# A streaming-encoder block on one core: 19 instead of 12 of 22 gate and up pairs by seven products

## The chip, the cores and the metric

The kernel runs on one core of a Trainium2 chip. A core has a matrix engine (TensorE, PE in the profile, with its weight loads as PEld), a vector engine (VectorE, DVE), an activation engine (ScalarE, ACT), a general engine (GpSimd, POOL) and a sync engine (SyncE, SP) that here only issues DMAs. Each engine runs its instructions in the order in which they stand in its queue. The metric is the device time of one execution in microseconds (us); the lower the better.

## The reference, cut to what matters

The block works on x, 512 tokens of 1024 channels, in float32. It has two token mixers side by side (a gated delta rule with 8 heads, and a convolution), an output projection with a residual, and a feed-forward part. The change concerns the last:

```
h2 = rmsnorm(x, norm2_w[l])
f_gate, f_up = jnp.split(h2 @ ffn_w_gate_up[l], 2, axis=-1)
x = x + (jax.nn.silu(f_gate) * f_up) @ ffn_w_down[l]
return rmsnorm(x, norm_f_w)
```

The hidden width is 2816, which is 22 tiles of 128. One tile of the gate and the tile of up with the same number make a "pair" f, from 0 to 21.

## The kernel before

**Products.** Every float32 weight is split into a high and a low part (`whi`, `wlo`): `unit` (L101) loads a weight tile into `raw` on SP's queue, copies it to `whi` on ScalarE (L111) and subtracts on VectorE to get `wlo` (L112). The activations are split likewise, so that one exact product is three matmuls, `split3` (L121). The tiles raw, whi and wlo have three buffers each (`wp`).

**Stages.** (1) To about 377 us: the input projections, one unit of 8 k blocks after another, with the work of the heads between them. For each head POOL runs a recursion of 15 steps (L502 and L504, tiles `ytm` and `y`) whose result ScalarE takes up at L557 (`YY<-y`) in a later chain of small matmuls. (2) To about 560 us the remaining projections of the mixers. (3) The output projection `tok_mm` (L918) in two halves, `hf` 0 and 1; in the second half it normalizes the token tiles n = 0 to 3 one by one (`norm2`, with two small POOL operations, L952 and L954, for each), and PE transposes them. (4) The gate and up pairs from about 596 to 829 us. (5) The down projection, `two` (L1213) three times and a tail.

**Pairs in two ways.** A pair below F0 = 10 is direct: 8 k blocks of 3 matmuls for the gate, as many for up, each with 512 columns, so 48 matmuls (`col_tile`, L123). A pair from F0 on goes through `pair` (L1129): the gate and up tiles, split in two along k, are four quarter blocks A11, A12, A21, A22; the activations are split in two along k and in two along the tokens; and the 2 x 2 block product is done with seven products of half blocks in place of eight (the scheme of Strassen and Winograd). Each product, `hprod` (L1120), is 4 k blocks of 3 matmuls with 256 columns, so a pair has 84 matmuls. It has four units, of 1024, 1024, 1024 and 512 columns, and writes four PSUM banks `z`. The banks come from two pools: `bank` (pool psw, name w, five banks) and `bank2` (pool psm, name mm, three banks); pairs take four of the first, or one of the first and three of the second, by turns.

**Sums of weights.** Three of the four units load sums of quarter blocks, s1 to s4, which the kernel makes itself in DRAM. For each sum SP issues a copy of a quarter (L192), and POOL issues a DMA that adds another quarter or sum onto it (L196, `accum_op=ALU.add`). The list `feed` holds the order; `feed_one` issues the next copy and, two copies later, the adding DMA. s2 adds s1, and s4 adds s2. `fill` (L200) is called from `unit` while `start_feed` is set: from step 335 of the heads' stage to the last three units of the output projection, and again from pair 1 on.

**Sums of activations.** `todo` (L1074) is a list of eleven steps that make the activation sums (tiles xb) and their high and low parts (th, tl). Two of them stand in each direct pair from f = 1 on (`next_todo`).

**Down sums.** The down projection goes by seven products as well; its weight sums `wsum` are added on POOL in SBUF. Those that are left after stage 3 (four whole ones) are made by `dsums_to` in the direct pairs with odd f: a load issued by POOL into `wst` (L166), four additions on POOL (L172), and a store (L173). `some_operands` splits the finished hidden tiles for the down projection (tiles fh, fl), and for f from 11 on POOL combines two of them (fm<-fm).

Of the kernel before, what the change touches and what calls it, by code (L numbers as in the profile page):

```python
# [20 lines left out]
FF = 22  # L21
# [11 lines left out]
def block_kernel(ctx, tc, a):  # L33
    nc = tc.nc
# [59 lines left out]
                    st.enter_context(tc.issue_after(i))  # L94
            yield

    loads, start_feed, gps_ = [], [False], []

    last = [None]

    def unit(ap, pool=None):  # L101

        aps = ap if isinstance(ap, tuple) else (ap,)
        n = T * len(aps) if isinstance(ap, tuple) else 1024
        raw, hi, lo = ((pool or wp).tile([P, n if pool else 1024], t, name=x)[:, 0:n]
                       for t, x in ((F32, "raw"), (F32R, "whi"), (F32R, "wlo")))
        for i, p in enumerate(aps):
            loads.append(nc.sync.dma_start(raw[:, i * T:(i + 1) * T] if len(aps) > 1 else raw, p))
        if start_feed[0]:
            fill()  # L110
        marked(S.activation(hi, raw, AF.Copy), "unit")  # L111
        marked(V.tensor_tensor(out=lo, in0=raw, in1=hi.bitcast(F32), op=ALU.subtract), "unit")  # L112
        return hi, lo
# [28 lines left out]
    cs = []  # L142
# [2 lines left out]

    FK, F0 = FF // 2, 10
    sums = {n: dram.tile([FF - F0, P, T], F32, name=n, bufs=1) for n in ("s1", "s2", "s3", "s4")}
    gu = {n: a["wgu"][r * FF + F0:(r + 1) * FF][:, :, c * T:(c + 1) * T]  # L150
          for n, r, c in (("A11", 0, 0), ("A12", 0, 1), ("A21", 1, 0), ("A22", 1, 1))}


    feed = [("s1", 0)] + [w for p in range(FF - F0) for w in (("s3", p), ("s2", p), ("s1", p + 1), ("s4", p))]
    feed = [(*w, *{"s1": ("A21", gu["A22"]), "s3": ("A11", gu["A21"]), "s2": ("A11", sums["s1"]),
                   "s4": ("A12", sums["s2"])}[w[0]]) for w in feed if w[1] < FF - F0]
    fed, begun = [], []
# [28 lines left out]
    def feed_one(n=1):  # L186

        for _ in range(n):
            if feed:
                w, p, m, other = feed.pop(0)  # L190
                with tc.issue_after(loads[-1].ins):
                    nc.sync.dma_start(sums[w][p], gu[m][p])  # L192
                begun.append((sums[w][p], other[p]))
        while len(begun) > (2 if feed else 0):
            with tc.issue_after((fed[-1] if fed else last[0]).ins):
                fed.append(nc.gpsimd.dma_start(*begun.pop(0), accum_op=ALU.add, max_dma_last_dim=2048))  # L196

    units, norming = [0], [False]
# [641 lines left out]
    queue.append(rest)  # L840
    nh = 0
    while step() or chains:
        start_feed[0] = count[0] >= 335
        if nh < H and count[0] >= START - 9 + 32 * nh + sum(OTHERS[:nh]):
            chains.append([0, chain(*done[nh])])
            nh += 1
        for c in list(chains):
            if c[0] <= count[0] or not queue:
                with behind():
                    n = next(c[1], None)  # L850
                if n is None:
                    chains.remove(c)
                else:
                    c[0] = count[0] + n
    background()
    for _, sc, e in ended:
        if not sc:
# [60 lines left out]
    def tok_mm(wname, kts, xh, xl, post, between):  # L918


        for hf in range(2):
# [11 lines left out]
            for kp2 in range(nu - tail):  # L933
                w = unit(a[wname][hf, kp2])
                for n in range(NT):
                    part(n, kp2, w)
            start_feed[0] = not hf
            ws = [unit(a[wname][hf, kp2]) for kp2 in range(nu - tail, nu)]
            cs = slice(hf * 512, hf * 512 + 512)
            for n in range(NT):  # L940
# [105 lines left out]
        tt(b[:, t1], b[:, t2], fm[:, t2], ALU.add, G)  # L1046

    def dsums_to(f):
        if f % 2 and rest:
            k, cs = rest.pop(0)  # L1050
            if rest and rest[0][0] == k:
                rest.pop(0)
                cs = slice(0, T)
            r = fs.tile([P, 4, T], F32, name="wst")[:, :, 0:cs.stop - cs.start]
            dsums_load(k, r, nc.gpsimd, cs)
            dsums_add(k, r, cs)


# [23 lines left out]
    def some_operands(f):  # L1082
        if not ff:
            fxs.close()
            ff.append(ctx.enter_context(tc.tile_pool(name="ff", bufs=FK)))
        for _ in range(3 if f < F0 else 2):
            if len(made) <= f:
                operands(len(made))
                made.append(1)

    def next_todo():
        if todo:
            with behind():
                todo.pop(0)()

    for f in range(F0):
        start_feed[0] = f > 0
        dsums_to(f)
        if f > 1:
            pg = psm.tile([P, T], F32, name="mm")  # L1100
            col_tile(pg, a["wgu"][f], hhk, hlk)
        else:
            pg = first[2 * f][0]
            k_loop(*first[2 * f], slice(2 * P, T))
        sg = fq.tile([P, T], F32, name="cw", bufs=2)
        S.activation(sg, pg, AF.Silu)
        if f:
            next_todo()
            pu = psm.tile([P, T], F32, name="mm")
            col_tile(pu, a["wgu"][FF + f], hhk, hlk)  # L1110
        else:
            pu = first[1][0]
            k_loop(*first[1], slice(2 * P, T))
        tt(hidden(), pu, sg, ALU.mult)
        if f:
            next_todo()
        if f > 6:
            some_operands(f)

    def hprod(ps, w, i, x):  # L1120

# [6 lines left out]

    def pair(f):  # L1129

        z = [bank() for _ in range(4)] if f % 2 == 0 else [bank(), bank2(), bank2(), bank2()]
        s = lambda n: sums[n][f - F0]
        w = unit(a["wgu"][f])
        w46 = unit((a["wgu"][FF + f][:, T:], s("s2")))
        hprod(z[0][:, t1], w, 0, B11)
        hprod(z[1][:, t1], w, 1, B21)
# [252 lines left out]
```

## Time and profile before

| | |
|---|---|
| three runs | 941.52, 942.86 (median), 943.43 us |
| the profiled execution | 943.44 us, span 941.7 us, granted clock 0.997 |
| PE busy | 925.4 us (98%), 4952 matmuls |
| VectorE, ScalarE, POOL busy | 740.8, 558.0, 336.8 us |
| moved by DMA | 177.39 MB |

The profile is of one execution. Its own time is 0.58 us above the median of the runs, and 1.7 us above its span. A busy PE in it means that a matmul is in flight; matmuls overlap, so the rate is read from the distance of one start to the next.

### The profile page before, as it was taken

The numbers are of one execution on the slowest core, as the hardware profiler recorded it, in microseconds if no ns is written. First come the engines' busy times: TensorE is split into PE (matmuls) and PEld (weight loads), VectorE is DVE, ScalarE is ACT, GpSimd is POOL, SyncE is SP. The second block draws the span as 40 slices with busy tenths as digits, with TensorE's granted clock in tenths as the row PEclk, the third lists the DMA queues.
The fourth block names the chain that finished last, engine by engine and source line by source line (L and its number), as shares of the span: only waits on it lengthen the run. The fifth ranks groups of instructions, "written<-read, shape, count | busy, mean of one in ns | idle before, by whom it ended". The sixth has DMA issues, their size and how long they took to land.

```text
span 941.7 us, 14545 instructions
## 1 busy us (share of the span) xinstructions
PE 925.4 (98%) x4952; PEld 785.3 (83%) x4952; DVE 740.8 (79%) x1157; ACT 558.0 (59%) x1278; POOL 336.8 (36%) x541
## 2 busy tenths in 40 slices
PE   9999999999999999999999999999999999999996
PEld 6777788878888888888888888988889999988885
DVE  4889898989989899999587643676536877888896
ACT  6696977888778796643555323324324445466545
POOL 0134345253353437544055341245531111133042
PEclk9999999999999999999999999999999999999999
DMA  9333413223123246989898983699797564577654
GB/s 322 113 114 118 131 68 103 86 85 108 73 77 103 93 136 159 335 263 268 284 286 279 285 236 127 205 292 288 257 257 213 184 197 168 186 236 255 213 181 148
DMA packets 78187, 177.39 MB, mean 188 GB/s; under 512 B 10080, under 2 KB 19472, under 8 KB 77088
## 3 DMA queue, kind: packets, MB, share of 16 engines
q1 hardware_dynamic: 66528, 144.89, 44.9%
q0 software_dynamic: 10288, 28.90, 13.3%
q10 hardware_dynamic: 1296, 2.67, 0.7%
q8 instruction: 39, 0.64, 0.3%
q14 instruction: 36, 0.29, 0.1%
HBM read 156.22 MB, written 45.37 MB: 214 GB/s over the span
## 4 chain that ended last, share of the span: by engine, by line
PE 82%; ACT 7%; DVE 3%; issue 1%; POOL 1%; DMA 1%; POOLq 0%; ACTq 0%; DVEq 0%; SPq 0%
PE mm L121 55%; PE w L121 20%; PE b L526 2%; DVE wlo L112 1%; ACT whi L111 1%; PE g L435 1%; PE g L470 1%; PE st L639 1%; PE st L630 1%; PE st L638 1%; PE st L624 1%; PE st L625 0%; ACT Un L473 0%; DVE xs L964 0%; PE b L435 0%
## 5 line engine op out<-in xcount | busy, mean ns | idle before, releaser
L111 ACT ACTIVATE whi<-raw 128x1024 fp32r<-128x1024 f32 (+1 forms) x191 | 196.4, 1030 | 242.6 <-PE mm L121 158.0
L112 DVE TENSOR_TENSOR wlo<-raw,whi 128x1024 fp32r<-128x1024 f32 (+1 forms) x191 | 239.6, 1256 | 86.1 <-ACT whi L111 84.8
L121 PE MATMUL mm<-hh,whi 128*128 128x512 f32 (+1 forms) x688 | 269.7, 392 | 1.2 <-ACT whi L111 0.8
L121 PE MATMUL mm<-hh,wlo 128*128 128x512 f32 (+1 forms) x688 | 264.2, 385 | 0.8 <-DVE wlo L112 0.8
L121 PE MATMUL mm<-hl,whi 128*128 128x512 f32 (+1 forms) x688 | 263.0, 382 | 0.0
L693 DVE SCALAR_TENSOR_TENSOR cps<-c,c31w,cps 128x512 f32<-128x512 f32 x224 | 167.9, 749 | 3.8
L121 PEld LDWEIGHTS mm<-hh,wlo 128*128 128x128 f32 x688 | 130.0, 189 | 25.0 <-DVE wlo L112 1.3
L121 PEld LDWEIGHTS mm<-hh,whi 128*128 128x128 f32 x688 | 130.3, 189 | 22.9 <-ACT whi L111 1.7
L121 PEld LDWEIGHTS mm<-hl,whi 128*128 128x128 f32 x688 | 130.3, 189 | 20.9
L1022 POOL TENSOR_TENSOR fm<-fm 128x256 f32<-128x256 f32 x33 | 28.1, 852 | 117.7 <-DVE s L1022 93.2
L422 DVE SCALAR_TENSOR_TENSOR acc<-mm,c4w,acc 128x511 f32<-128x511 f32 (+2 forms) x72 | 53.0, 740 | 4.3 <-ACT acc L419 4.1
L502 POOL TENSOR_TENSOR ytm<-U,y 128x60 f32<-128x60 f32 (+14 forms) x120 | 36.7, 306 | 51.0 <-DMA U<-sc 42.2
L121 PE MATMUL mm<-yh,whi 128*128 128x512 f32 x128 | 50.6, 396 | 0.0
L121 PE MATMUL mm<-yh,wlo 128*128 128x512 f32 x128 | 49.8, 389 | 0.0
L121 PE MATMUL mm<-yl,whi 128*128 128x512 f32 x128 | 49.8, 389 | 0.0
L121 PE MATMUL w<-hh,wlo 128*128 128x256 f32 x168 | 47.7, 284 | 0.3 <-DVE wlo L112 0.3
L121 PE MATMUL w<-hh,whi 128*128 128x256 f32 x168 | 47.6, 284 | 0.0
L121 PE MATMUL w<-hl,whi 128*128 128x256 f32 x168 | 47.5, 283 | 0.0
L196 POOL DMA_DIRECT2D s<-in_wgu_dram x24 | 22.7, 962 | 64.0 <-DMA s<-in_wgu_dram 64.0
L121 PE MATMUL w<-wlo,fh 128*128 128x512 f32 (+1 forms) x115 | 44.3, 385 | 0.2 <-DVE wlo L112 0.2
L121 PE MATMUL w<-whi,fl 128*128 128x512 f32 (+1 forms) x115 | 44.2, 385 | 0.0
L121 PE MATMUL w<-whi,fh 128*128 128x512 f32 (+1 forms) x115 | 44.2, 385 | 0.0
(346 smaller groups left out, 1937.5 us busy)
## 6 DMA issues: line engine op xcount, KB each, us to landing
raw<-in_win_dram SPq DMA_DIRECT2D x61, 512.0 KB, 3.2
raw<-in_wgu_dram SPq DMA_DIRECT2D x32, 512.0 KB, 3.2
s<-in_wgu_dram SPq DMA_DIRECT2D x48, 256.0 KB, 5.3
raw<-s SPq DMA_DIRECT2D x48, 256.0 KB, 3.6
raw<-wsum SPq DMA_DIRECT2D x44, 256.0 KB, 3.6
raw<-in_wdn_dram SPq DMA_DIRECT2D x33, 256.0 KB, 3.2
s<-in_wgu_dram POOLq DMA_DIRECT2D x24, 256.0 KB, 6.8
s<-s POOLq DMA_DIRECT2D x24, 256.0 KB, 7.2
```

The source lines that it names most:

```text
L111: marked(S.activation(hi, raw, AF.Copy), "unit")
L112: marked(V.tensor_tensor(out=lo, in0=raw, in1=hi.bitcast(F32), op=ALU.subtract), "unit")
L121: marked(PE.matmul(ps, l, r, start=first and i == 0, stop=last and i == 2))
L196: fed.append(nc.gpsimd.dma_start(*begun.pop(0), accum_op=ALU.add, max_dma_last_dim=2048))
L422: marked(V.scalar_tensor_tensor(out=acc[:, s:], in0=ps[:, :T - s], scalar=c4w[:, j, k:k + 1], in1=acc[:, s:], op0=ALU.mult, op1=ALU.add))
L435: PE.transpose(ps[:, n, :], src[:, n, :], ident)
L470: PE.matmul(ps[:, n, :], kT[:, n, :], kT[:, n, :], start=True, stop=True)
L502: G.tensor_tensor(out=tm[:, :, 0:w], in0=U[:, k, :, k + 1:], in1=y[:, :, k:k + 1].broadcast_to([P, NT, w]), op=ALU.mult)
L526: PE.matmul(ps[:, q, 0:w], stationary[:, q, :], moving[:, q, :], start=True, stop=True)
L624: PE.matmul(ps[:, 0, :], kT[:, n, :], Sp, start=True, stop=True)
L693: V.scalar_tensor_tensor(out=acc if k < 30 else cv[i], in0=c[:, k:k + T], scalar=c31w[:, i, k:k + 1], in1=acc if k > 1 else cv[i], op0=ALU ...
L1022: return eng.tensor_tensor(out=out, in0=in0, in1=in1, op=op)
```

## The change

F0 goes from 10 to 3: the pairs 3 to 9 go by seven products too, 19 pairs in all. Around that:

- The list of weight sums grows from 48 to 76. Its order takes two pairs by turns (s3 of two, s2 of two, s1 of the next two, s4 of two). It is issued from step 72 of the heads' stage on, one sum at each unit (`ahead`), and with the last three units of the output projection and those of pair 0 as well.
- Each call of `next_todo` does two steps, with calls in the direct pairs 0 to 2 and one in each `pair`.
- The down sums that are left stand behind pairs 8, 11, 14 and 17.
- The turns of the PSUM banks count from F0, so that the last pair takes four banks of pool w; before, it took one of w and three of mm.

```diff
+        elif ahead[0]:
+            feed_one()
...
-    FK, F0 = FF // 2, 10
+    FK, F0 = FF // 2, 3
...
-    feed = [("s1", 0)] + [w for p in range(FF - F0) for w in (("s3", p), ("s2", p), ("s1", p + 1), ("s4", p))]
+    feed = [("s1", 0), ("s1", 1)] + [(n, p + d + i) for p in range(0, FF - F0, 2)
+                                     for n, d in (("s3", 0), ("s2", 0), ("s1", 2), ("s4", 0)) for i in range(2)]
...
-            with tc.issue_after((fed[-1] if fed else last[0]).ins):
+            with tc.issue_after(fed[-1].ins) if fed else nullcontext():
...
+        ahead[0] = count[0] >= 72
         start_feed[0] = count[0] >= 335
...
-            start_feed[0] = not hf
+            start_feed[0], ahead[0] = not hf, hf
...
-        if f % 2 and rest:
+        if f > 7 and f % 3 == 2 and rest:
...
-            dsums_load(k, r, nc.gpsimd, cs)
+            with tc.issue_after(loads[-1].ins):
+                dsums_load(k, r, nc.gpsimd, cs)
...
-        for _ in range(3 if f < F0 else 2):
+        for _ in range(2):
...
-        if todo:
+        for _ in todo[:2]:
             with behind():
                 todo.pop(0)()
...
-        if f:
-            next_todo()
-        if f > 6:
-            some_operands(f)
+        next_todo()
...
-        z = [bank() for _ in range(4)] if f % 2 == 0 else [bank(), bank2(), bank2(), bank2()]
+        z = [bank() for _ in range(4)] if (f - F0) % 2 == 0 else [bank(), bank2(), bank2(), bank2()]
...
+        next_todo()
```

What this does to the queues is shown at three places. The first is POOL's queue in the heads' stage, between the recursion of head 0 and that of head 1, before (L464 to L486 make the tiles from which the recursion of head 1 starts):

```order
L504 TENSOR_TENSOR y_720<-y_720,ytm_764 128x4
L464 TENSOR_TENSOR ss_1005<-ss_1005,root4_85 128x4
L474 TENSOR_TENSOR Un_1029<-Un_1029,DT_663 128x512
L481 COPY cp_1035<-Un_1029 32x128 x4
L484 TENSOR_SCALAR cc_1036<-cp_1035,cst_76 128x64
L485 TENSOR_SCALAR ct_1037<-cp_1035,cst_76 128x64
L486 TENSOR_TENSOR cc_1036<-cc_1036,ct_1037 128x64
```

The same place after:

```order
L507 TENSOR_TENSOR y_720<-y_720,ytm_764 128x4
L199 DMA s1_125<-in_wgu_dram 128x512 x2
L199 DMA s3_127<-in_wgu_dram 128x512
L467 TENSOR_TENSOR ss_1005<-ss_1005,root4_85 128x4
L199 DMA s3_127<-in_wgu_dram 128x512
L477 TENSOR_TENSOR Un_1029<-Un_1029,DT_663 128x512
L199 DMA s2_126<-s1_125 128x512
L484 COPY cp_1035<-Un_1029 32x128 x4
L487 TENSOR_SCALAR cc_1036<-cp_1035,cst_76 128x64
L488 TENSOR_SCALAR ct_1037<-cp_1035,cst_76 128x64
L489 TENSOR_TENSOR cc_1036<-cc_1036,ct_1037 128x64
L199 DMA s2_126<-s1_125 128x512
```

Six adding DMAs now stand among the steps that lead to the next recursion; in all, 35 of the 76 stand in the heads' stage ahead of the place where POOL's first down sum stood.

The second place is POOL's queue in the second half of the output projection: ss2 is the tile of `norm2`, and the first four of its eight TENSOR_SCALARs belong to the first half. Before:

```order
L952 TENSOR_SCALAR ss2_6029<-ss2_6029 128x1 x5
L954 TENSOR_TENSOR ss2_6029<-ss2_6029,half_81 128x1
L952 TENSOR_SCALAR ss2_6029<-ss2_6029 128x1
L954 TENSOR_TENSOR ss2_6029<-ss2_6029,half_81 128x1
L952 TENSOR_SCALAR ss2_6029<-ss2_6029 128x1
```

After:

```order
L957 TENSOR_SCALAR ss2_6093<-ss2_6093 128x1 x3
L199 DMA s2_126<-s1_125 128x512
L957 TENSOR_SCALAR ss2_6093<-ss2_6093 128x1
L199 DMA s1_125<-in_wgu_dram 128x512
L957 TENSOR_SCALAR ss2_6093<-ss2_6093 128x1
L959 TENSOR_TENSOR ss2_6093<-ss2_6093,half_81 128x1
L199 DMA s1_125<-in_wgu_dram 128x512
L957 TENSOR_SCALAR ss2_6093<-ss2_6093 128x1
L959 TENSOR_TENSOR ss2_6093<-ss2_6093,half_81 128x1
```

Three adding DMAs stand among these, the last of them between token tiles 0 and 1 of the second half.

The third place is PE's queue where the last pair ends and the down projection begins, with what each matmul waits for. The mm or w with 256 columns is the last product of pair 21; the four w with 512 columns are the first four accumulators of the down projection. Before:

```order
L121 MATMUL mm_8747<-hh_92,wlo_8835 128x256
L121 MATMUL w_8889<-whi_8894,fh_7101 128x512 [waits Activation_49]
L121 MATMUL w_8889<-whi_8894,fl_7102 128x512
L121 MATMUL w_8889<-wlo_8895,fh_7101 128x512 [waits DVE_49]
L121 MATMUL w_8890<-whi_8894,fh_7101 128x512
L121 MATMUL w_8890<-whi_8894,fl_7102 128x512
L121 MATMUL w_8890<-wlo_8895,fh_7101 128x512
L121 MATMUL w_8891<-whi_8894,fh_7101 128x512 [waits PE_49]
```

After:

```order
L123 MATMUL w_9223<-hh_92,wlo_9311 128x256
L123 MATMUL w_9365<-whi_9370,fh_6935 128x512 [waits Activation_49]
L123 MATMUL w_9365<-whi_9370,fl_6936 128x512
L123 MATMUL w_9365<-wlo_9371,fh_6935 128x512 [waits DVE_49]
L123 MATMUL w_9366<-whi_9370,fh_6935 128x512 [waits DVE_49]
L123 MATMUL w_9366<-whi_9370,fl_6936 128x512
L123 MATMUL w_9366<-wlo_9371,fh_6935 128x512
L123 MATMUL w_9367<-whi_9370,fh_6935 128x512 [waits DVE_49]
```

Pool w has five banks. With four of them in the last pair, the second, third and fourth accumulator of the down projection take over banks of that pair, and each now waits for VectorE to have read its bank.

3 lines of the change are left out of this document (2 added, 1 removed).

## The prediction

> **What bounds the kernel now.** I read the page first, then the busy time by stage (windows), then PE's timeline at the ends of stages, then the waits.
>
> ```profile
> span 941.7 us, 14545 instructions
> ...
> PE 925.4 (98%) x4952; PEld 785.3 (83%) x4952; DVE 740.8 (79%) x1157; ACT 558.0 (59%) x1278; POOL 336.8 (36%) x541
> ...
> PE 82%; ACT 7%; DVE 3%; issue 1%; POOL 1%; DMA 1%; POOLq 0%; ACTq 0%; DVEq 0%; SPq 0%
> ```
>
> PE is busy 98% of the span, and 82% of the chain that ended last is PE's. The windows are the heads' stage, the end of the output projection with pair 0, the direct pairs 2 to 9, and the pairs 10 to 21 of seven products (columns: length, then busy time of PE, PEld, DVE, ACT, POOL, then clock, DMA share, GB/s):
>
> ```profile
> 44.00:377.00 333.00, 327.03 (x1716) 270.43 (x1717) 300.20 (x566) 270.48 (x821) 145.94 (x343) 0.99 0.33 105
> 560.00:615.00 55.00, 54.68 (x324) 48.33 (x323) 29.43 (x36) 19.49 (x34) 11.13 (x19) 1.00 0.52 167
> 620.80:707.80 87.00, 87.00 (x385) 72.09 (x384) 47.14 (x42) 27.77 (x37) 38.36 (x37) 1.00 0.91 278
> 707.80:828.80 121.00, 121.00 (x1010) 120.96 (x1009) 92.72 (x139) 59.53 (x83) 17.01 (x22) 1.00 0.60 190
> ```
>
> In the two windows of pairs PE never waits. What happens there is worth its matmuls, as long as the others keep up: VectorE has (121.00 - 92.72) / 12 = 2.4 us to spare in a pair of seven products.
>
> **The gain.** PE's timeline has the first matmul of pair 2, of pair 10, of pair 15, of the down projection, and of its third accumulator:
>
> ```profile
> 620.79 0.39 PE L121 MATMUL mm<-hh,whi 128*128 128x512 f32 x1
> 707.83 0.28 PE L121 MATMUL w<-hh,whi 128*128 128x256 f32 x1
> 758.23 0.28 PE L121 MATMUL w<-hh,whi 128*128 128x256 f32 x1
> 828.78 0.40 PE L121 MATMUL w<-whi,fh 128*128 128x512 f32 x1
> 830.17 0.39 PE L121 MATMUL w<-whi,fh 128*128 128x512 f32 x1
> ```
>
> Eight direct pairs take 707.83 - 620.79 = 87.04 us, 10.88 each: 48 matmuls at 0.227 us. Twelve pairs of seven products take 828.78 - 707.83 = 120.95 us, 10.08 each: 84 matmuls at 0.120 us. Not an eighth is gained but 0.80 us of 10.88, since a matmul of half the columns takes more than half the time. Seven pairs change over: 7 x 0.80 = **-5.6 us**, all of it on PE's path.
>
> Each of the 84 needs a weight load of its own, and that is longer than its step:
>
> ```profile
> L121 PEld LDWEIGHTS w<-hh,whi 128*128 128x128 f32 x168 | 32.2, 192 | 0.0
> ```
>
> A load of 192 ns is shown for each 120 ns of matmul, so loads lie beside matmuls and beside each other. [...]
>
> **The bank at the end of the pairs.** The last pair now has four banks of pool w, and the down projection's second to fourth accumulator take them over. VectorE reads them in pair 21 at these times (the sum of z[2], then of z[1]):
>
> ```profile
> 830.04 0.68 DVE L1022 TENSOR_TENSOR fm<-mm,cv 128x512 f32<-128x512 f32 x1
> 830.64 0.68 DVE L1022 TENSOR_TENSOR cw<-cw,mm 128x512 f32<-128x512 f32 x1
> ```
>
> The third accumulator starts at 830.17 now, and its bank is then z[1], read out at 830.64 + 0.68 = 831.32. PE waits 831.32 - 830.17 = **+1.15 us**. The second takes z[0], which was read long before; the fourth takes z[2], free at 830.72, before PE comes to it. No other work of PE is queued ahead, so nothing hides this.
>
> **Down sums beside pairs of seven.** Nothing that the order shows holds POOL's first `wst` load back to pair 8, and I expect POOL to run the four blocks about when it does now: the first beside pairs 0 and 1, the other three at 636, 655 and 676 us, now beside pairs of seven products. Rows of POOL's and VectorE's timelines, two such blocks, then two operations beside the first of them and one with POOL idle:
>
> ```profile
> 613.40 8.00 POOL L172 TENSOR_TENSOR wst<-wst 128x512 f32<-128x512 f32 x4 [1.22 <-DMA wst<-in_wdn_dram]
> ...
> 676.27 6.33 POOL L172 TENSOR_TENSOR wst<-wst 128x512 f32<-128x512 f32 x4 [7.49 <-DMA wst<-in_wdn_dram]
> ```
> ```profile
> 613.66 2.11 DVE L112 TENSOR_TENSOR wlo<-raw,whi 128x1024 fp32r<-128x1024 f32 x1
> 615.70 2.32 DVE L1022 TENSOR_TENSOR xb<-xb,xb 128x1024 f32<-128x1024 f32 x1
> ...
> 755.13 1.23 DVE L112 TENSOR_TENSOR wlo<-raw,whi 128x1024 fp32r<-128x1024 f32 x1 [0.68 <-ACT whi L111]
> ```
>
> A subtraction for wlo takes 2.11 beside POOL's additions and 1.23 alone, 0.9 more; the xb of 615.70 takes 1.1 more than the one of 605.41 that is quoted below. A block of 6.3 to 8.0 us has room for four such operations of VectorE: 0.9 + 3 x 1.1 = 4.2 us lost. Two things cover that: the 2.4 us that VectorE has to spare in a pair, of which 1.9 lie in the block's 8 of 10 us; and its lead, since the wlo of 755.13 is done at 756.36 and PE comes to its pair at 758.23, 1.9 us, and to the matmul that reads wlo two steps of 0.12 later, 2.1. So a block costs 4.2 - 1.9 - 2.1 = 0.2 us. Bounds: 0 if only three operations meet a block, 4.2 - 2.1 = 2.1 a block if the spare time lies elsewhere. For three blocks **+0.6 us**, between 0 and 6.3; nearer to 0, since the spare time is there in every pair.
>
> **The eleven steps of todo**, pressed from six pairs into three. Four joins, four sums and three subtractions at 1.2 us (the xb of 605.41 below) are 13.5, with the first `wst` block 17.7. Beside them VectorE has five wlo (6.2), two fm (1.4) and two fl (0.8) before pair 3 begins at 620.79 + 48 x 0.227 = 631.7.
>
> ```profile
> 605.41 1.22 DVE L1022 TENSOR_TENSOR xb<-hh,hl 128x1024 f32<-128x1024 f32 x1
> 657.39 5.58 DVE L1019 TENSOR_TENSOR fl<-fm,fh 128x256 fp32r<-128x256 f32 x5 [0.48 <-ACT fh L1018]
> ```
>
> With those, 17.7 + 6.2 + 1.4 + 0.8 = 26.1 us of work in 631.7 - 605.4 = 26.3 us: just full. The first of the tiles is read in the third product, 24 x 0.12 = 2.9 us into the pair, which is the cover that is left. I take **+0.3 us**, a little over one more block's worth, between 0 and 2. Without that cover it would be 2.9 more.
>
> **Adding DMAs among POOL's work.** 35 come into the heads' stage, five a head. Their price now, over 48, with POOL's longest wait for a copy, and the slack of the recursion: its last `y` and ScalarE's taking it up, for the heads 1, 3 and 7 (1 has the smallest slack of the heads 1 to 7; the other four lie above that of head 3):
>
> ```profile
> L196 POOL DMA_DIRECT2D s<-in_wgu_dram x24: 800/894/1715, 361.0 to 706.0; - x24
> ```
> ```profile
> POOL s L196 <- DMA s<-in_wgu_dram: 77.6, 16, 13.1
> ```
> ```profile
> 125.10 0.21 POOL L504 TENSOR_TENSOR y<-y,ytm 128x4 f32<-128x4 f32 x1
> ...
> 204.40 0.21 POOL L504 TENSOR_TENSOR y<-y,ytm 128x4 f32<-128x4 f32 x1
> ...
> 358.82 0.21 POOL L504 TENSOR_TENSOR y<-y,ytm 128x4 f32<-128x4 f32 x1
> ```
> ```profile
> 140.97 0.34 ACT L557 ACTIVATE YY<-y,cst 128x64 f32<-128x64 f32 x1
> ...
> 224.38 0.33 ACT L557 ACTIVATE YY<-y,cst 128x64 f32<-128x64 f32 x1
> ...
> 376.29 0.35 ACT L557 ACTIVATE YY<-y,cst 128x64 f32<-128x64 f32 x1
> ```
>
> Five calls at 0.9 us are 4.5 us a head, or 8.6 at 1.7 each, against slacks of 140.97 - 125.31 = 15.7, 19.8 and 17.3 us. POOL has 333 - 146 us free there. So they are hidden: 0. The order of the other engines in this stage is shuffled by it, and PE's idle 333.00 - 327.03 = 6.0 us may move by a third either way: +-2, taken as 0. DMAs are no bound there (share 0.33).
>
> Of the sums, 14 pairs' worth stand ahead of the last normalization in POOL's queue, so pair 3 finds its own, and SP does not wait.
>
> In the output projection's second half one adding DMA stands ahead of token tile 1's normalization:
>
> ```profile
> 587.38 0.30 POOL L952 TENSOR_SCALAR ss<-ss 128x1 f32<-128x1 f32 x1 [3.06 <-ACT sg L950]
> ```
> ```profile
> 579.73 0.33 SPq L108 DMA_DIRECT2D raw<-in_wgu_dram  x1
> ```
> ```profile
> s<-in_wgu_dram SPq DMA_DIRECT2D x48, 256.0 KB, 5.3
> ```
>
> Its copy follows the weight load of 579.73 on SP, so it is issued at 580.1 and lands 5.3 later; POOL's call ends at 586.3, 1.1 us ahead of need: 0, up to 3 if the copy is late.
>
> **Sum.** -5.6 + 1.15 + 0.6 + 0.3 = -3.55 us. Against the profiled 943.44 that is 939.9; the runs' median lies 0.58 lower, so the forecast is 942.86 - 3.55 = **939.3 us**. 0.2% of this time is 1.9 us, about what a measurement can tell from no change.
>
> **Rivals.**
> - *The cover holds everywhere*: neither the down sums nor todo cost PE anything, and the heads' stage loses a little of its idle time: -5.6 + 1.15 - 1 = -5.5, 937.4 us. For it: VectorE's spare time. Chance 0.14; faster.
> - *VectorE becomes the bound in pairs 3 to 8*: the blocks cost half of their bound of 6.3, 3.2 in place of 0.6, and todo 1: -5.6 + 1.15 + 3.2 + 1 = -0.25, 942.6. For it: 26.1 of 26.3 us. Against: one block in three pairs. Chance 0.16, of it 0.13 same and 0.03 slower.
> - *POOL's recursion comes late* (the other side): each of the heads 1 to 7 meets one wait of 13.1 us and calls of 1.7, 21.6 us. It decides from a head's slack on: 5.9 us at head 1, 4.3 at head 7 and 1.8 at head 3; with 0 to 1.8 at the other four, taken as 0.5 each, 14.0 in all. -3.55 + 14.0 = +10.45, 953.3. Against it: a copy is issued two sums ahead of its adding. Chance 0.09; slower.
> - [...] Chance 0.01.
>
> The forecast has 0.60: 0.57 faster, 0.03 same. That makes faster 0.71, same 0.16, slower 0.13. The range goes from below the second case, 936.5, to just above the third, 943.0; what is left out is the fourth, the fifth, and the slower part of the third and some way below 936.5.
>
> **What would show it.** Nineteen pairs at 10.08 us each with PE always busy; PE waiting about 1.15 us for VectorE's cw at the down projection's third accumulator; PE waiting for wlo, if at all, beside POOL's `wst`; ScalarE's `YY` never waiting for POOL. It is wrong if a pair of seven in 631 to 707 takes over 10.4 us, if PE's idle time in the heads' stage grows by over 2 us, or if the transposes of token tile 1 wait for POOL.

## The result, and the profile after

The changed kernel takes 956.39 us (median of 4 runs, 956.05 to 957.72), the kernel before 942.80 beside it (941.52 to 943.43): a ratio of 1.0149, interval [1.0131, 1.0166]. It is slower by about 14 us; the prediction was 3.5 us faster.

The page of the changed kernel (first the span, then busy time by engine, then the chain of waits):

```profile
span 954.9 us, 15285 instructions
...
PE 927.7 (97%) x5204; PEld 797.6 (84%) x5204; DVE 767.6 (80%) x1206; ACT 567.8 (59%) x1297; POOL 365.1 (38%) x569
...
PE 67%; ACT 7%; DVE 7%; DMA 6%; issue 4%; POOL 3%; SPq 0%; POOLq 0%; ACTq 0%; DVEq 0%
```

PE's share of the chain falls from 82% to 67%, and VectorE, DMAs and "issue" take what it lost. PE does not have more to do (927.7 us for 925.4); it waits. Where, PE's timeline tells: the first matmul of the output projection, of the gate and up stage, and of the down projection, first before, then after.

```profile
461.37 0.39 PE L121 MATMUL mm<-yh,whi 128*128 128x512 f32 x1
...
596.36 0.36 PE L121 MATMUL w<-hh,whi 128*128 128x256 f32 x1
```
```profile
467.19 0.39 PE L123 MATMUL mm<-yh,whi 128*128 128x512 f32 x1
...
603.04 0.36 PE L123 MATMUL w<-hh,whi 128*128 128x256 f32 x1
...
842.62 0.40 PE L123 MATMUL w<-whi,fh 128*128 128x512 f32 x1
```

The heads lose 467.19 - 461.37 = 5.8 us; the output projection with the normalization 0.9 (135.85 us for 134.99); the gate and up stage takes 842.62 - 603.04 = 239.6 us, where it took 828.78 - 596.36 = 232.4, so 7.2 are lost where 5.6 were to be gained. The down projection is 0.6 shorter. Before rounding that is 13.2 us in all, the difference of the two spans.

The windows of the changed kernel: the heads' stage, the stretch with the loss in the pairs, and the pairs behind it.

```profile
44.00:377.00 333.00, 323.29 (x1694) 267.91 (x1693) 294.65 (x560) 264.35 (x812) 168.63 (x367) 0.99 0.55 150
...
640.00:710.00 70.00, 63.27 (x482) 61.21 (x482) 47.23 (x61) 26.79 (x39) 27.55 (x24) 0.95 0.86 276
...
710.00:840.00 130.00, 130.00 (x1086) 130.00 (x1085) 102.21 (x154) 64.99 (x91) 15.33 (x20) 1.00 0.55 186
```

From 710 us on PE never waits: the gain is real there. Between 640 and 710 us PE has 482 matmuls where the 130 us behind it have 1086 (585 in 70 us), the granted clock is 0.95, and the DMA engines are busy 0.86 at 276 GB/s, against 0.55 at 186 behind. Those are the pairs 3 to 8 with the down sums of GpSimd (called POOL in the profile) beside them.

Who waits there: ScalarE, which makes whi, for loads of the pairs' sums (three figures: us in total, times, longest), and how long those loads take from issue to landing. Both rows are of 640 to 710 us.

```profile
ACT whi L113 <- DMA raw<-s: 23.2, 9, 6.0
```
```profile
raw<-s SPq DMA_DIRECT2D x23, 256.0 KB, 6.1
```

### The profile page after: what moved, and what is told of

The parts are those of the page before. It is cut to its first block, busy times and chain, and to the rows that moved or that the text cites. A ratio compares the mean times of both kernels' runs of the same rounds, so it can differ in the third digit from the quotient of the medians.

```text
span 954.9 us, 15285 instructions
## 1 busy us (share of the span) xinstructions
PE 927.7 (97%) x5204; PEld 797.6 (84%) x5204; DVE 767.6 (80%) x1206; ACT 567.8 (59%) x1297; POOL 365.1 (38%) x569
## 4 chain that ended last, share of the span: by engine, by line
PE 67%; ACT 7%; DVE 7%; DMA 6%; issue 4%; POOL 3%; SPq 0%; POOLq 0%; ACTq 0%; DVEq 0%
PE mm L123 40%; PE w L123 21%; DMA raw<-s 4%; DVE wlo L114 3%; PE b L529 2%; ACT whi L113 2%; DVE cps L696 1%; DMA s<-in_wgu_dram 1%; POOL ytm L505 1%; DVE acc L425 1%; PE st L642 1%; PE g L438 1%; PE st L641 1%; PE st L633 0%; DMA DT<-mrow 0%
## 5 line engine op out<-in xcount | busy, mean ns | idle before, releaser
L114 DVE TENSOR_TENSOR wlo<-raw,whi 128x1024 fp32r<-128x1024 f32 (+1 forms) x205 | 256.3, 1251 | 80.8 <-ACT whi L113 79.7
L123 PE MATMUL mm<-hh,whi 128*128 128x512 f32 (+1 forms) x612 | 237.5, 389 | 2.0 <-ACT whi L113 1.5
L123 PE MATMUL mm<-hh,wlo 128*128 128x512 f32 (+1 forms) x612 | 231.5, 378 | 0.9 <-DVE wlo L114 0.9
L123 PE MATMUL mm<-hl,whi 128*128 128x512 f32 (+1 forms) x612 | 229.8, 375 | 0.0
L123 PE MATMUL w<-hh,wlo 128*128 128x256 f32 x244 | 70.4, 289 | 1.8 <-DVE wlo L114 1.7
L123 PE MATMUL w<-hh,whi 128*128 128x256 f32 x244 | 69.9, 287 | 1.1 <-ACT whi L113 1.1
L123 PE MATMUL w<-hl,whi 128*128 128x256 f32 x244 | 69.6, 285 | 0.0
L199 POOL DMA_DIRECT2D s<-s x38 | 34.2, 901 | 48.1 <-DMA s<-in_wgu_dram 47.0
L505 POOL TENSOR_TENSOR ytm<-U,y 128x60 f32<-128x60 f32 (+14 forms) x120 | 40.8, 340 | 30.2 <-DMA s<-in_wgu_dram 11.3
L123 PEld LDWEIGHTS w<-hh,wlo 128*128 128x128 f32 x244 | 47.5, 195 | 2.8 <-DVE wlo L114 2.6
L123 PEld LDWEIGHTS w<-hh,whi 128*128 128x128 f32 x244 | 47.5, 195 | 1.4 <-ACT whi L113 1.3
```

Of the source, the lines that this page charges most:

```text
L123: marked(PE.matmul(ps, l, r, start=first and i == 0, stop=last and i == 2))
L505: G.tensor_tensor(out=tm[:, :, 0:w], in0=U[:, k, :, k + 1:], in1=y[:, :, k:k + 1].broadcast_to([P, NT, w]), op=ALU.mult)
```

## The experiments

All fourteen kernels in one table. The first two columns are read off PE's timeline of one profiled execution, in us: the start of the output projection, and the length of the gate and up stage. The last is the ratio of the timed runs to those of the kernel before on the same chip. The heads of e1, e2, e6, e7, e9 and e10 are those of the changed kernel and gave 463.3 to 467.2 in single executions, so the first column alone tells differences of some 4 us and up; the ratio stands beside it. The changed kernel's own 5.8 us are not far above that; the ratio of e5 below is the better figure for the heads.

| kernel | output projection | gate and up | ratio, 95% |
|---|---|---|---|
| before | 461.4 | 232.4 | |
| after | 467.2 | 239.6 | 1.0149 [1.0131, 1.0166] |
| e1 no down sums | 466.5 | 227.2 | 1.0002 [0.9987, 1.0017] |
| e2 down sums late, SyncE's queue | 465.6 | 228.3 | 1.0028 [1.0012, 1.0043] |
| e3 no early feed | 459.9 | 274.9 | 1.0477 [1.0455, 1.0498] |
| e4 lag of five | 467.4 | 238.8 | 1.0143 [1.0127, 1.0159] |
| e5 power put back | 458.3 | 238.4 | 1.0070 [1.0057, 1.0083] |
| e6 early, SyncE's queue | 465.5 | 238.9 | 1.0117 [1.0102, 1.0132] |
| e7 late, GpSimd's queue | 466.4 | 240.5 | 1.0182 [1.0167, 1.0197] |
| e8 = e2 + e5 | 458.5 | 231.9 | 0.9981 [0.9965, 0.9996] |
| e9 = e7 without the adds | 467.2 | 231.1 | 1.0044 [1.0022, 1.0066] |
| e10 = e7, adds alone | 463.3 | 227.4 | 1.0028 [1.0014, 1.0041] |
| e11 = e8 with half blocks | 458.2 | 228.5 | 0.9943 [0.9925, 0.9960] |
| e12 six direct pairs + e5 | 458.9 | 229.2 | 0.9952 [0.9935, 0.9969] |

**e1: without the down sums.**

```diff
-        if f > 7 and f % 3 == 2 and rest:
+        if False:
...
-    wt = lambda k, i: wsum[k][:, {1: 1, 2: 0, 3: 3, 4: 2}[i], :]
+    left_out = {k for k, _ in rest}
+    wt = lambda k, i: wd(k, i - 1) if k in left_out else wsum[k][:, {1: 1, 2: 0, 3: 3, 4: 2}[i], :]
```

> The changed kernel with the down sums of the pairs left out: the blocks that were summed beside the pairs (a load of 1 MB, four adds on GpSimd, a store of 1 MB each) are not made, and the down projection reads unsummed weights in their place, so this part of the output is not the reference's. Theory (the lost time of the gate and up stage, 12.8 us over what its steps add up to, is loads that land late behind the down sums' transfers at 276 GB/s in 640 to 710 us): ScalarE's wait for raw sums, 30.1 us in 14 now, falls under 6 us, the stage from the first gate product to the first down product falls from 239.6 to 227 to 230 us, and the run takes 944 to 947 us. Rival (the transfers of the pairs' own sums, or units that are asked for just in time, are enough by themselves): the waits stay over 20 us and the run takes 952 us or more. The heads stay late by 5.8 us by both.

```profile
640.00:710.00 70.00, 70.00 (x586) 70.00 (x585) 49.59 (x74) 34.02 (x47) 4.06 (x5) 1.00 0.70 213
```
```profile
raw<-s SPq DMA_DIRECT2D x28, 256.0 KB, 3.6
```

PE is full, loads of sums land in 3.6 us in place of 6.1, and the stage takes 227.2 us, 5.2 less than before. The theory holds: the seven pairs gain what the prediction said, and the four blocks of down sums cost 239.6 - 227.2 = 12.4 us. ScalarE's wait for sums falls from 30.1 us to 5.5. The time, 941.94 us, lies 2 us under the expected range.

**e2: the load on SyncE's queue.**

```diff
-                dsums_load(k, r, nc.gpsimd, cs)
+                dsums_load(k, r, nc.sync, cs)
```

> One queue changed: the down sums' load is issued by SyncE, behind the weights of its pair, and no longer by GpSimd, so the four loads really stand behind pairs 8, 11, 14 and 17, about 30 us apart and from about 690 us on. Theory (the transfers collide because they run early and close together while the last sums of the pairs are still being made): the stage takes 229 to 233 us in place of 239.6 and the run 946 to 950 us. Rival (the amount of traffic beside the pairs counts, not when it runs): the waits move with the loads, and the run stays at 954 to 958 us. Second rival: the load waits in SyncE's queue for its buffer, and the next pair's weights wait behind it: over 958 us.

The four loads are now issued at 685, 715, 746 and 777 us, and the stage takes 228.3 us: 11.3 of the 12.4 us are back. So the blocks as such can be had for about 1 us. The stage and the time, 943.98 us, both lie a little under the expected ranges. But this edit changes two things, the queue and the time; e6 and e7 are the other two corners.

**e3: no early feed.**

```diff
-        ahead[0] = count[0] >= 72
```

> The sums of the pairs are not begun in the heads: they start at step 335, as in the kernel before, all else as changed. Theory (the heads' 5.8 us come from GpSimd waiting at an adding DMA for its copy, with the decay matrix's add behind it): the first product of the output projection is back at 461 to 462 us (467.2 now). The sums then run on far into the pairs, with the down sums beside them, so the gate and up stage loses as much as now or more (240 to 250 us): the run takes 950 to 962 us. Rival for the heads (three pairs fewer and other pools shift the heads, not the adding DMAs): the output projection still begins after 465 us.

```profile
640.00:800.00 160.00, 130.15 (x935) 123.70 (x934) 89.95 (x128) 54.97 (x78) 53.40 (x58) 0.93 0.99 282
```

The heads are back at 459.9 us, so their loss does come with the early feed. What it costs later was missed by far: with the sums of the pairs, the weights and the down sums together the DMA engines are busy 0.99 at 282 GB/s for 160 us, and PE works 130 of 160. The early feed is needed; its side effect in the heads is not.

**e4: a greater lag.**

```diff
-        while len(begun) > (2 if feed else 0):
+        while len(begun) > (5 if feed else 0):
```

> One number changed: an adding DMA is issued five copies behind its own, no longer two, so that the copy has landed when GpSimd reaches the add. Theory (GpSimd waits there, 107.0 us in 30, and holds the decay matrix's add and with it ScalarE and TensorE): the waits of the adding DMAs for their copies fall to under a third, the 4 us gap of TensorE at 167 us goes, the output projection begins at 461.5 to 463.5 us, and the run takes 951 to 953.5 us, the later stage unchanged. Rival (the heads lose to the transfers themselves, at twice the share of the DMA engines): the waits fall, but the output projection still begins after 465.5 us and the run takes 955 us or more.

Nothing moved, the waits that it was to take away least of all. The row of the changed kernel, then of this one, from 44 to 462 us:

```profile
POOL s L199 <- DMA s<-in_wgu_dram: 58.2, 18, 8.6
```
```profile
POOL s L199 <- DMA s<-in_wgu_dram: 60.0, 18, 9.3
```

GpSimd still waits there as long, and the 4 us gap of PE stayed. The run did not take away what it was to take away, so it speaks neither for my theory nor against it. What GpSimd does before the gap shows another candidate. Its timeline in the changed kernel, and in the kernel before:

```profile
140.22 0.92 POOL L199 DMA_DIRECT2D s<-s  x1 [0.22 <-issue]
153.23 1.05 POOL L662 TENSOR_TENSOR ss<-ss,half 128x4 f32<-128x4 f32 x1 [12.09 <-DVE ss L660]
154.26 0.28 POOL L505 TENSOR_TENSOR ytm<-U,y 128x60 f32<-128x60 f32 x1
...
167.32 0.21 POOL L507 TENSOR_TENSOR y<-y,ytm 128x4 f32<-128x4 f32 x1
167.79 0.85 POOL L199 DMA_DIRECT2D s<-in_wgu_dram  x1 [0.26 <-issue]
168.32 1.16 POOL L199 DMA_DIRECT2D s<-s  x1
168.88 1.88 POOL L447 TENSOR_TENSOR DT<-DT,cst 128x512 f32<-128x512 f32 x1
```
```profile
147.97 0.29 POOL L502 TENSOR_TENSOR ytm<-U,y 128x60 f32<-128x60 f32 x1 [7.07 <-DMA U<-sc]
...
160.11 0.21 POOL L504 TENSOR_TENSOR y<-y,ytm 128x4 f32<-128x4 f32 x1
160.27 1.04 POOL L659 TENSOR_TENSOR ss<-ss,half 128x4 f32<-128x4 f32 x1
161.28 1.29 POOL L444 TENSOR_TENSOR DT<-DT,cst 128x512 f32<-128x512 f32 x1
```

The small power `ss<-ss,half` (the output scale of a finished head, of four columns) stands behind the recursion before the change and ahead of it after. There it waits 12.09 us for VectorE, with the recursion queued behind it, whose input has long come (its last load is issued at 144.6 us and lands 3.1 us later). The recursion ends at 167.5 in place of 160.3, two adding DMAs come on top, and the add on the decay matrix DT ends at 170.8. ScalarE's exponentials on DT stand ahead of `w` in its queue, and PE waits for `w`:

```profile
167.45 0.39 PE L123 MATMUL mm<-hl,whi 128*128 128x512 f32 x1
171.50 0.79 PE L641 MATMUL st<-w,kd 128*128 128x128 f32 x2 [3.66 <-ACT w L635]
...
173.37 0.63 PE L123 MATMUL mm<-hl,whi 128*128 128x512 f32 x1
173.80 0.63 PE L123 MATMUL mm<-hh,wlo 128*128 128x512 f32 x1
174.23 0.63 PE L123 MATMUL mm<-hh,whi 128*128 128x512 f32 x1
```

**e5: that one operation put back** behind the recursion, the adding DMAs all as they are.

```diff
-        tc.keep_in_program_order(G.tensor_tensor(out=ss[:, 4], in0=ss[:, 3], in1=half4, op=ALU.pow))
+        with tc.issue_after(last[0].ins):
+            tc.keep_in_program_order(G.tensor_tensor(out=ss[:, 4], in0=ss[:, 3], in1=half4, op=ALU.pow))
```

> One small operation put back: GpSimd's power for a head's output scale (the first of its kind, which the changed kernel has ahead of head 2's recursion and the kernel before behind it) is again behind the recursion in GpSimd's order; the adding DMAs all stay. New theory of the heads, after the run with five copies of lag moved nothing: that operation waits 12.1 us for VectorE, the recursion behind it starts at 153.3 us instead of 147, ends at 167.5, and the decay matrix's add, ScalarE's exponentials and TensorE come behind it. Then the 4 us gap at 167 us and the slow products behind it go, the output projection begins at 460.5 to 462 us (467.2 now) and the run takes 949.5 to 952 us, the rest unchanged. Rival (the adding DMAs themselves hold GpSimd, 0.9 us each, or the transfers slow the loads): still after 465 us.

```profile
158.31 0.21 POOL L507 TENSOR_TENSOR y<-y,ytm 128x4 f32<-128x4 f32 x1
158.47 1.04 POOL L663 TENSOR_TENSOR ss<-ss,half 128x4 f32<-128x4 f32 x1
...
162.63 1.39 POOL L447 TENSOR_TENSOR DT<-DT,cst 128x512 f32<-128x512 f32 x1 [0.18 <-DMA DT<-mrow]
```

The recursion ends at 158.5, the gap is gone, and the output projection begins at 458.34 us, 8.9 earlier. By the ratios it is (1.0149 - 1.0070) x 942 = 7.4 us, more than the 5.8 that the heads had lost, and the normalization is back at 135.0 us as well. The new theory holds; the adding DMAs themselves cost the heads nothing that shows (459.9 us in e3, which has none of the early ones). The heads and the run, 948.37 us, both lie under the expected ranges: the heads are 3 us shorter than in the kernel before. Most of these 3 us belong to the one profiled execution of the kernel before and not to the edit: it is 1.0 us behind e5 already at 44 us, and from 76.7 to 79.2 us its matmuls step at 427 ns, at a granted clock of 0.61 (77 to 80 us), which with a wait of 0.82 us ahead of it makes 1.6 us more by 90 us. So 5.8 us is likely too low for the loss in the heads.

**e6 and e7: the two other corners.** e6 has the load on SyncE, but early; e7 has it on GpSimd behind a copy that really waits for the pair.

```diff
-        if f > 7 and f % 3 == 2 and rest:
+        if f < 8 and f % 2 and rest:
...
-                dsums_load(k, r, nc.gpsimd, cs)
+                dsums_load(k, r, nc.sync, cs)
```

> Down sums' loads on SyncE's queue as in the run before, but early again: behind the weights of gate 1 and of pairs 3, 5 and 7, which is where GpSimd ran them by itself. It tells the time from the queue. Theory A (crowding: the blocks collide with the last sums of the pairs between 640 and 710 us, whatever queue the load is on): the stall is back, 9 us or more of the 12, the gate and up stage takes 237 us or more and the run 952 to 958 us. Theory B (GpSimd's queue: a load of 1 MB that GpSimd issues lands in the way of the weights, or the last adding DMAs stand behind it): the stage takes 228 to 231 us and the run 943 to 947 us.

```diff
-            with tc.issue_after(loads[-1].ins):
+            mk = fs.tile([P, 1], F32, name="mk", bufs=2)
+            with tc.issue_after(G.tensor_copy(out=mk, in_=fms[f][:, 0:1]).ins):
                 dsums_load(k, r, nc.gpsimd, cs)
```

> The other corner: the load stays on GpSimd's queue, but a one-column copy on GpSimd that reads pair f's hidden tile stands ahead of it, so that it really comes behind pairs 8, 11, 14 and 17 (about 690, 720, 751 and 781 us), behind all adding DMAs. Theory A (crowding in time): the stage takes 227 to 230 us, as with SyncE's late loads, and the run 942.5 to 946 us. Theory B (GpSimd's queue as such slows the weights): stalls at each of the four places, 232 us or more, the run 947 us or more.

```profile
640.00:710.00 70.00, 63.09 (x485) 61.33 (x484) 49.97 (x62) 27.35 (x39) 24.36 (x21) 0.95 0.86 273
```
```profile
700.00:826.00 126.00, 117.47 (x940) 114.73 (x939) 103.64 (x132) 54.38 (x79) 45.27 (x44) 0.99 0.68 231
```

Early on SyncE (first row) the stall is back in full, 238.9 us, with the same clock and DMA share as in the changed kernel. Late on GpSimd (second row) it has moved to the four new places, 240.5 us. Each of theories A and B has one run for it and one against: of these four corners only the blocks that came late and in SyncE's own row of loads were cheap. In e2 a block's load lands in 5.3 us (median) and the next weights are issued behind it; in e7 it takes 6.7 beside them. One difference is left between the two late corners: e7's loads are issued at 702, 734, 768 and 802 us, 17 to 25 us after e2's, since the copy waits for the end of the pair. Whether the queue or this other place in the pairs makes the stall is not shown.

**e8: both mends.** The edits of e2 and e5.

> The two mends together: the down sums' load on SyncE behind pairs 8, 11, 14 and 17, and the power behind the recursion. If both losses are independent and named rightly, the run is what the prediction's sum made of it without its two added terms: 943.9 less 4 to 6 us, 937 to 940 us, faster than the kernel before by 2 to 5 us, TensorE at 10.08 us a pair. Rival (the mend of one uncovers another wait, so the gains do not add): 941.5 us or more.

938.60 us beside 941.36 before: faster, and inside the expected 937 to 940. But the gate and up stage takes 231.9 us where e2's took 228.3, by waits of up to 1.2 us for wlo. The gains add in direction and not in full: over the 227.2 us without them, the four late blocks cost 1.1 us in e2 and 4.7 in e8. Both are single executions, and the one of e8 took 940.86 us, 2.3 above the median of its twelve. The ratios tell of the same shortfall, about 3 us: the gains of e2 and e5 would add up to 0.9949, and e8 has 0.9981.

**e9 and e10: a block's transfers and its adds apart**, in the place of e7. e9 takes out the four adds. e10 keeps them, on one tile filled once, and moves 16 KB in place of each 1 MB:

```diff
-            dsums_add(k, r, cs)
+            nc.gpsimd.dma_start(wsum[k][:, :, cs], r)
```
```diff
-            r = fs.tile([P, 4, T], F32, name="wst")[:, :, 0:cs.stop - cs.start]
...
+            r, few = alone[0], slice(0, 8)
...
-                dsums_load(k, r, nc.gpsimd, cs)
-            dsums_add(k, r, cs)
+                dsums_load(k, r[:, :, few], nc.gpsimd, few)
...
+                for o, x, y in ((b22, b12, b22), (b12, b11, b12), (b11, b22, b11), (b21, b11, b21)):
+                    G.tensor_tensor(out=o, in0=x, in1=y, op=ALU.add)
+            nc.gpsimd.dma_start(wsum[k][:, :, few], r[:, :, few])
```

> The down sums late on GpSimd's queue, as in the run that lost at each of its four places, without the four adds of each block: the loads and stores of 1 MB stay, so the weights reach the down projection unsummed and that part of the output is not the reference's. It tells a block's adds from its transfers; the gate and up stage took 240.5 us with both and 227.2 us with neither. Theory (the adds on GpSimd slow VectorE's split beside them, 1.22 us to about 2 us, at a place where VectorE is 80 per cent busy): the stage takes 227 to 231 us. Rival (the transfers make the weights land late): 236 us or more.

> The other half: the four adds of each block at the same four places, without their transfers (16 KB are loaded and stored in place of 1 MB each, and the down projection reads unsummed weights, so that part of the output is not the reference's). Theory (the adds slow VectorE): the stage takes 234 us or more, with splits of about 2 us beside the adds. Rival (the transfers): 227 to 230 us. If both halves alone stay under 231 us, it takes the two together.

VectorE's splits from 700 to 826 us (number, busy us, mean ns of one, idle before), with neither (e1), with the transfers (e9), with the adds (e10), with both (e7):

```profile
L114 DVE TENSOR_TENSOR wlo<-raw,whi 128x1024 fp32r<-128x1024 f32 (+1 forms) x50 | 54.2, 1084 | 18.8 <-ACT whi L113 18.8
```
```profile
L114 DVE TENSOR_TENSOR wlo<-raw,whi 128x1024 fp32r<-128x1024 f32 (+1 forms) x49 | 55.1, 1124 | 22.7 <-ACT whi L113 21.7 <-PE w L123 0.7 <-PE mm L123 0.3
```
```profile
L114 DVE TENSOR_TENSOR wlo<-raw,whi 128x1024 fp32r<-128x1024 f32 (+1 forms) x50 | 61.3, 1226 | 11.0 <-ACT whi L113 10.6 <-PE mm L123 0.3
```
```profile
L114 DVE TENSOR_TENSOR wlo<-raw,whi 128x1024 fp32r<-128x1024 f32 (+1 forms) x46 | 57.4, 1249 | 16.9 <-ACT whi L113 16.9
```

Over the 227.2 us with neither, the transfers alone cost 3.9 us, the adds alone 0.2, both 13.3. The 3.9 are an upper bound: 1.2 of them are lost before e9's first block is issued, and the profiled execution of e9 is the slowest of its five, 3.7 us above their median. The profiled execution of e10 is 3.2 us under the median of its eight; its heads, which do not enter this stage, are 3 to 4 us shorter than those of e7 and e9. By any of these figures the two halves cost far less apart than together. My theory of these two runs, that the adds do it, falls; so does the rival. The adds slow the splits by 13% and VectorE makes it up (its idle time goes from 18.8 to 11.0 us). The transfers make ScalarE wait for late loads, 32.8 us in e9 and 6.7 in e10 in this window, and VectorE, idle meanwhile, makes up for much of that too. With both, the late split is also a slow one, and PE waits: for wlo 6.6 us in ten waits in e7, 1.5 in three in e9, 0.3 in one in e10. The two were taken apart in the late place and on GpSimd's queue only; that the early stall is made in the same way is an inference from its late loads and from the same adds.

**e11: half blocks.** e8 with each block cut in two, behind pairs 5, 7, 9 and so on.

```diff
-        if f > 7 and f % 3 == 2 and rest:
+        if f > 4 and f % 2 and rest:
             k, cs = rest.pop(0)
-            if rest and rest[0][0] == k:
-                rest.pop(0)
-                cs = slice(0, T)
-            r = fs.tile([P, 4, T], F32, name="wst")[:, :, 0:cs.stop - cs.start]
+            r = fs.tile([P, 4, 256], F32, name="wst")
```

> The two mends, with the down sums in eight half blocks behind every other pair from pair 5 on, in place of four whole ones: 0.5 MB and four adds of half the length each, so that no pair has more than about 3 us of adds beside it. If a block costs because its 6 us of adds exceed the pair's slack on VectorE (10.08 us less about 8), the stage takes 227 to 229 us and the run 934 to 937.5 us. Rival (the blocks cost by their sum, however they are cut): 938 to 942 us.

936.64 us beside 941.83, a ratio of 0.9943 [0.9925, 0.9960]: 5.4 us faster than the kernel before, inside the expected 934 to 937.5. The stage takes 228.5 us; whole blocks on the same queue gave 228.3 (e2) and 231.9 (e8), so the halves are as good as the better of these, and the ratio's interval lies below that of e8. Three of the halves are issued at 650, 669 and 689 us, in the stretch of the early stall, and PE has no wait there, with the DMA engines busy 0.82 at 254 GB/s. So a half block on SyncE's queue need not come late. e11 has the power put back and e6 has not, and in this stretch e11 issues 1.5 to 2 MB of such loads and e6 2 MB, so the size of the blocks is the likely reason, but it was not changed alone.

Not all of the 5.4 us come from the pairs. In the profiled executions e11 is 6.6 us shorter than the kernel before: 3.2 by the heads, 3.9 by the gate and up stage and 0.7 by the down projection, less 1.3 for the normalization.

**e12: six direct pairs**, sixteen of seven products, the blocks beside the direct pairs 1, 2, 4 and 5, and the power put back.

```diff
-    FK, F0 = FF // 2, 3
+    FK, F0 = FF // 2, 6
...
-        if f > 7 and f % 3 == 2 and rest:
+        if f in (1, 2, 4, 5) and rest:
```

> Six direct pairs in place of three and sixteen of seven products, with the power put back and the four blocks of down sums beside the direct pairs 1, 2, 4 and 5, where the kernel before has them. Expected: the heads as in the run with the power put back, 458.4 us to the output projection, the blocks hidden as before, and four pairs at 0.80 us less than the kernel before: 941.4 less 3.0 less 3.2, 933.5 to 937 us. Rival (even there the blocks and the pairs' sums collide): 938 us or more.

```profile
595.00:822.00 227.00, 227.00 (x1700) 218.44 (x1700) 168.17 (x224) 101.19 (x142) 49.39 (x46) 1.00 0.60 198
```

PE is full over the whole stage: 229.2 us, which is 232.4 less 4 x 0.80 to the tenth. 938.07 us beside 941.83. The run lies 1 us above the 933.5 to 937 that I expected. The heads are short again, 458.9 us; but the 3 us of that sum were read against the profiled execution of the kernel before, 943.44 us, and taken off a median of 941.4, 2 us less.

## Why the prediction was wrong

Two steps failed by most: the price of a block of down sums (0.6 us in all, measured 12.4), and the order of the queues in the heads (0, measured 5.8). Term by term:

- **Gain, -5.6: right.** Without the down sums the stage is 5.2 us shorter, which is -5.6 and the 0.3 for todo and its like. No run shows the case with the chance of 0.01, that weight loads hold PE back: from 710 us on they take 192 ns each in the changed kernel, and its pairs have PE busy without a gap at steps of 0.120 us, as the twelve had.
- **Todo, +0.3: the size fits**, as far as 227.2 - (232.4 - 5.6) = 0.4 us tells it; that it is todo's was not taken apart. "SP does not wait" for sums holds too: pair 3's were begun at 89 us, its loads at 625.
- **Bank, +1.15: not there.** The third accumulator follows without a wait; the fourth, at 844.71, and its second matmul are about 0.1 us late together:

```profile
843.32 0.40 PE L123 MATMUL w<-whi,fh 128*128 128x512 f32 x1
843.55 0.39 PE L123 MATMUL w<-whi,fl 128*128 128x512 f32 x1
843.78 0.39 PE L123 MATMUL w<-wlo,fh 128*128 128x512 f32 x1
844.01 0.39 PE L123 MATMUL w<-whi,fh 128*128 128x512 f32 x1
...
844.71 0.47 PE L123 MATMUL w<-whi,fh 128*128 128x512 f32 x1
```

  "Its bank is then z[1]" was the step that failed. VectorE reads z[1] until 845.16 in this run, so the accumulators have the other three. That the banks were handed over in the order in which they came free is read from these times only.
- **Down sums, +0.6 (at most 6.3): 12.4.** When the blocks would run it had about right: their adds begin at 620, 642, 666 and 688 us, in a stage that begins 6.7 us later than before. The step "a block costs 4.2 - 1.9 - 2.1 = 0.2 us" fails. It priced VectorE's slower operations alone, and e10 shows that part to be small, as it said, though in the late place: 0.2 us for all four blocks. It had no term for a block's transfers, though a row in the prediction had the direct pairs at a DMA share of 0.91 with the blocks and the sums beside them, and another the pairs of seven at 0.60 with hardly either. A pair of seven loads 1.75 MB in 10.08 us where a direct one loads 1 MB in 10.88. As far as e7, e9 and e10 show it, the covers that I counted, spare time and lead, were spent twice: once on the slow splits, once on the late loads. The sign that I had named is there too: by VectorE's last operation of each pair, the pairs 4, 5 and 6 take 14.3, 12.6 and 14.1 us, above the 10.4 that was named.
- **Adding DMAs in the heads, 0: 5.8** (7.4 by the ratio of e5). The calls are hidden, as said, and YY never waited. What failed is "The order of the other engines in this stage is shuffled by it", with "+-2, taken as 0". The shuffle was GpSimd's own: one operation that waits 12 us passed a recursion. I had priced the recursion's slack up to YY; the reader that was late was another, the add on DT behind it in the same queue. The rival of a late recursion had the right engine and the wrong reader. The sign that I had named, idle time of PE in the heads' stage up by over 2 us, is there: 9.7 for 6.0.
- **Normalization, 0 (up to 3): 0.9**, and between 0 and 1.3 in single executions of the other runs, so it is not told from 0.

Sum of the terms as measured, in the profiled execution: -5.2 + 12.4 + 5.8 + 0.9 - 0.6 = 13.3 us (13.2 before rounding). With both losses mended (e11) the change is faster, by 5.4 us where the forecast had 3.5. That the two are so near is in part luck: of the forecast's own terms the gate and up stage gives 3.9 us in place of 4.7, the bank's +1.15 is not there, and 3.2 us come from heads that the forecast took as unchanged.

## What to carry to other kernels

Work moved from one place to another is to be priced in every resource of the new place at once: its transfers beside those that are there, and its slow-down of other engines, against one and the same slack: here the adds of the four blocks alone cost 0.2 us and the transfers alone at most 3.9, and the two together 13.3. Where a scheduler sets the order, adding instructions to one queue can move others in it; look through the order of that queue for a short operation with a long wait that has passed a long one (here one of 1.05 us that waited 12.09), and price the wait for everything behind it. The mends were an order written down for one instruction, and blocks loaded in SyncE's row of weights, cut in half (a stage of 228.5 us); whole blocks there did as well in one of two kernels (228.3 and 231.9).

## What the runs showed of the hardware

**PE's clock was halved after some waits, and not after others like them.** After the heads' wait of 3.66 us the clock granted in 171.4 to 176.0 us is 0.50, and matmuls of 512 columns step at 427 ns in place of 227:

```profile
171.40:176.00 4.60, 4.50 (x13) 3.73 (x14) 1.15 (x3) 3.53 (x11) 0.12 (x1) 0.50 0.66 107
...
660.60:664.20 3.60, 2.82 (x13) 2.62 (x14) 3.36 (x5) 1.29 (x2) 0.00 (x0) 0.67 1.02 365
```

In the pairs it came after much shorter waits (second row, 0.67 in the mean): PE idle for 1.13 us and, 1.3 us on, for 0.76 us, then steps of 0.213 us in place of 0.120 until 665.2.

The length of a wait does not tell it alone. The same wait of the heads in e10, 3.69 us, is followed by the full clock:

```profile
169.61 0.49 PE L641 MATMUL st<-w,kd 128*128 128x128 f32 x2 [3.69 <-ACT w L635]
```
```profile
170.00:174.00 4.00, 4.00 (x23) 3.36 (x23) 2.47 (x6) 3.94 (x13) 0.00 (x0) 1.00 0.65 107
```

And waits of 0.47 and 0.82 us near 75 us are followed by 0.61 (77 to 80 us) in the kernel before, waits of 0.50 and 1.74 us near 692 us by 1.00 (693.5 to 697.1 us) in the changed kernel. What decides it, these runs do not show. By estimate it is one reason why the same heads (463.3 to 467.2 us) differ by up to 4 us from one execution to the next: 4.6 us at a clock of 0.50 are 2.3 us of matmuls lost.

**Three kernels with a tile of one column have a down projection that is 2 to 3% slower.** In e7, e9 and e10, which alone have the 4-byte tile `mk`, the matmuls of the down projection step at 0.23 to 0.24 us where those of e2 step at 0.22 to 0.23, without any wait and at a granted clock of 1.00 in both; e10, then e2:

```profile
850.02 0.39 PE L123 MATMUL w<-wlo,fh 128*128 128x512 f32 x1
...
852.35 0.39 PE L123 MATMUL w<-whi,fh 128*128 128x512 f32 x1
```
```profile
849.88 0.39 PE L123 MATMUL w<-whi,fh 128*128 128x512 f32 x1
...
852.15 0.39 PE L123 MATMUL w<-whi,fl 128*128 128x512 f32 x1
```

Ten steps take 2.33 us in the one and 2.27 in the other. From 845 to 930 us each of the three has 366 matmuls, the changed kernel 374 and e2 375. That the tile is the cause is a guess; it was not tried. The slower stage (8 or 9 matmuls fewer in that window, at 0.23 us) adds by estimate about 2 us to the ratios of these three kernels and nothing to their gate and up stage.
